# A shared PSUM bank in a seven-product down projection, and two transpose runs moved together in a stick-breaking head

## The chip, the cores and the metric

The kernel runs on one core of a Trainium2 chip. The metric is the device time of one execution, in microseconds (us). The core has TensorE (PE, matrix products and transposes, into the eight banks of PSUM), VectorE (DVE), ScalarE (ACT), GpSimd (POOL) and SyncE (SP, which issues the DMAs here). Each engine works through its own list of instructions in order and waits on semaphores for the others.

## The reference, cut to what matters

A decoder trunk of two layers, 512 tokens (T) of width 1024 (D), all in fp32. Each layer is FFN, mixer, FFN; the mixer of the first layer is a gated linear attention (GLA), that of the second a stick-breaking attention (SB).

```python
def swiglu(h, w_gate, w_up, w_down):
    return (silu(h @ w_gate) * (h @ w_up)) @ w_down      # 1024 -> 2816 -> 1024

def sb_mixer(h, w_in, w_out):            # 16 heads of 64
    q, k, v = split(h @ w_in, 3)
    # per head and block of 128 queries; mask is strictly causal
    z = (q_blk @ k.T) * scale
    sp = where(mask, softplus(z), 0)
    rem = reverse_cumsum(sp) - sp
    weights = where(mask, exp(log_sigmoid(z) - rem), 0)
    o = weights @ v
    return o @ w_out

for i in range(2):
    x = x + 0.5 * swiglu(rmsnorm(x), ...)
    x = x + mixer[i](rmsnorm(x))
    x = x + 0.5 * swiglu(rmsnorm(x), ...)
return rmsnorm(x)
```

## The kernel before, in words

**Number format.** A product in fp32 is made of three products of a shorter format. Each operand is split into a high half (a cast on ACT, `wh`, L129) and a low half (the rest, a subtraction on DVE, `wl`, L130); PE adds high by high, low by high and high by low into the same PSUM bank. Activations are split in the same way (`hh` and `hl`, L790 and L791; `xh` and `xl`).

**Layout.** x lies with features on the partitions, as eight tiles of 128 by 512. All eight PSUM banks are in one pool, under four tags with 2, 3, 2 and 1 banks (`a`, `z`, `t`, `o`). `psum(name)` without a tag (L46) goes round these eight in a fixed order, one turn for each call; `psum(name, tag)` takes the next bank of that tag. A bank that is taken again has to wait until its last reader is done.

**The order of the work.** The phases are FFN, GLA, FFN, FFN, SB, FFN. Weight products are entries of one queue, `feed`; an entry's body is a generator that yields at points where other work may be placed, and `feed.step(n)` goes on by n such points. Starting an entry also splits the weights of up to two further entries and asks for loads up to five ahead (`raw` and `rawd` are the tiles that a DMA from DRAM fills, two buffers each). On top of the order in the program text, a list scheduler places each engine's instructions; so an edit can move instructions that it doesn't name.

**FFN.** A part of the gate and up projections uses seven products of half size in place of eight (`seven`, product at L693). Its results pass through DVE: among others, the gate is multiplied in from PSUM (L706, `o <- ps_w, o`), then the result is split (L790, L791). A copy of a partial sum (`u`, L736) is made on ACT.

**Down by seven.** Two of the groups of 512 hidden features in each FFN (`DOWN_SEVEN = (1, 3)`) use seven products for the down projection too, in `seven_down` (L332 to 429). Each call makes a part (256 columns at two places) of the output; there are two parts in each group, so 16 calls in the four FFNs. Every product goes by `prod` (matmul at L372): two blocks of 128 by three, six matmuls with 256 columns, for each of two values of m. `add` (L376 to 378) adds the half of a finished sum into x, on DVE, straight from PSUM. `body_1` makes in this order: the products `b11` into two banks `ps_w`, and copies of them into two banks `ps_z` (ACT, L390); then `t1` into two banks `ps_q` (L391 to 394), with an `add` after each; then `t2`, `b21`. `body_2` adds `t3` to `ps_w`, `b22` to `ps_q` with an `add` after each, and `t4` to `ps_w`.

**SB.** `run` (L1394 to 1432) goes through 17 steps s, of which each does three things for heads, with steps of `feed` between them, an entry's step being for example twelve products of 512 columns (`ps_f`).

- `weights_log` for head s: in three blocks, the scores into `ps_z` (L1319, tag `z`), then on ACT Abs (L1338), Exp and Ln (`act`, L586) and Relu (L1341), on DVE a reverse scan (L1344) and a subtraction from `ps_z` (`r`, L1352). One `feed` step stands after the second block.
- `weights` for head s - 1 (L1355 to 1372): ten transposes of 128 by 128 (L1366) in three runs of 4, 4 and 2, each into a bank `ps_T` (tag `t`, two banks), each followed by an Exp on ACT that makes `wt` (L586). I call these exponentials exp a, b and c, and the runs T4, T4 and T2. A `feed` step stands after the first run and after the second, as long as the step has any left.
- `values` (L1374 to 1392), at every second step, for the pair of heads: 16 products into `ps_oT` (L1381) from the `wt` of both heads, a cast `oh` (L1390) and a subtraction `ol`.

ACT also splits the queries and keys of the next pair of heads (`mq`, L1292, and `kh`, L1303, from `n`).

Of the kernel before, what the change touches and what calls it, by code (L numbers as in the profile page):

```python
# [32 lines left out]
def decoder(ctx: ExitStack, tc: tile.TileContext, a: dict, out: bass.AP):  # L33
# [13 lines left out]
    def psum(name, tag=None):  # L47
        if tag is None:
            tag = order[turn_[0] % 8]
            turn_[0] += 1  # L50
        return pp.tile([P, T], F32, tag=tag, bufs=banks[tag], name=name)
# [284 lines left out]
    def seven_down(pool, w, r0, hs, part):  # L336

        H = T // 2  # L340
        lower, upper = (
            Chunk(w[r0 : r0 + 4 * P, c : c + 256].rearrange("(f p) c -> p f c", p=P), 4, 256)
            for c in (part * 256, 512 + part * 256)
        )
        lower.few = upper.few = True
        v = {}

        def halves():

            lo, up = (c.load().rearrange("p (c two) d -> p two c d", two=2) for c in (lower, upper))  # L350
            return lo[:, 0], lo[:, 1], up[:, 0], up[:, 1]

        def sums_12(_):
            a11, _, a21, a22 = halves()
            s = v["s12"] = pool().tile([P, 4, 256], F32, tag="s", bufs=4, name="s12")
            nc.vector.tensor_tensor(out=s[:, 0:2], in0=a21, in1=a22, op=ALU.add)
            nc.vector.tensor_tensor(out=s[:, 2:4], in0=s[:, 0:2], in1=a11, op=ALU.subtract)
            return s

        def sums_34(_):  # L360
            a11, a12, a21, _ = halves()
            s = pool().tile([P, 4, 256], F32, tag="s", bufs=4, name="s34")
            nc.vector.tensor_tensor(out=s[:, 0:2], in0=a11, in1=a21, op=ALU.subtract)
            nc.vector.tensor_tensor(out=s[:, 2:4], in0=a12, in1=v["s12"][:, 2:4], op=ALU.subtract)
            return s

        def prod(ps, w, k0, m, b, first):
            for c in range(2):
                bh, bl = hs[c][b]
                wh, wl = (t[:, k0 + c, m * P : (m + 1) * P] for t in w)  # L370
                for n, (l_, r_) in enumerate(((wh, bh), (wl, bh), (wh, bl))):
                    st["pe"] = nc.tensor.matmul(  # L372
                        ps, l_, r_, start=first and c + n == 0, stop=c == 1 and n == 2, skip_group_check=True
                    ).ins

        def add(m, up, col, ps):  # L376
            x = xs[part * 2 + m + 4 * up][:, col * H : col * H + H]
            nc.vector.scalar_tensor_tensor(out=x, in0=ps, scalar=0.5, in1=x, op0=ALU.mult, op1=ALU.add)

        def body_1(W):  # L380
            a11, s, v["a2"] = W
            ws, zs, qs = [], [], []
            for m in range(2):
                ws.append(psum("ps_w")[:, 0:H])
                prod(ws[m], a11, 0, m, "b11", True)
            for m in range(2):


                zs.append(psum("ps_z")[:, 0:H])
                nc.scalar.copy(zs[m], ws[m])  # L390
            yield  # L391
            for m in range(2):
                qs.append(psum("ps_q")[:, 0:H])
                prod(qs[m], s, 0, m, "t1", True)
                add(m, 1, 1, qs[m])
            yield
            for m in range(2):
                prod(ws[m], s, 2, m, "t2", False)
                add(m, 0, 1, ws[m])
            yield  # L400
            for m in range(2):
                prod(zs[m], v["a2"], 0, m, "b21", False)
                add(m, 0, 0, zs[m])
            v["w"], v["q"] = ws, qs
            yield

        def body_2(W):
            (s,) = W
            ws, qs = v["w"], v["q"]

            u3 = pool().tile([P, 2, H], F32, tag="c", bufs=1, name="u3")
            for m in range(2):
                prod(ws[m], s, 0, m, "t3", False)
                nc.scalar.copy(u3[:, m], ws[m])
                add(m, 1, 1, u3[:, m])
            yield
            for m in range(2):
                prod(qs[m], s, 2, m, "b22", False)
                add(m, 0, 1, qs[m])
            yield  # L420
            for m in range(2):
                prod(ws[m], v["a2"], 2, m, "t4", False)
                add(m, 1, 0, ws[m])
            yield

        units = [(lower, lambda t: halves()[0], 2, 256), (lower, sums_12, 4, 256), (lower, lambda t: halves()[1::2], 4, 256)]
        feed.q.append(Entry(units, body_1, NEAR, feed.q[-1].place != NEAR))
        assert not feed.q[-1].lead
        feed.q.append(Entry([(lower, sums_34, 4, 256)], body_2, NEAR))
# [55 lines left out]
    def stats_a(tag=None):  # L485

        if st["ss"] is None:
            sums = st["sums"]
        else:
            ps = psum("ps_st", tag)  # L490
            for i in range(NT):
                mm(ps[:, i : i + 1], st["ss"][:, i * P : (i + 1) * P], ones[:, 0:1], True, True)
            sums = ps[:, 0:NT]
        st["r4"] = rstd(sums, NT)
# [27 lines left out]
    def stats_b(tag=None):  # L522

        ps = psum("ps_R", tag)
        dgs = sp.tile([P, T], F32, tag="ss", name="dg")
        for i in range(NT):
            dg = dgs[:, i * P : (i + 1) * P]
            nc.vector.tensor_scalar(
                out=dg, in0=ident, scalar1=st["r4"][:, i : i + 1], scalar2=None, op0=ALU.mult
            )  # L530

            nc.tensor.matmul(
                ps[:, i * P : (i + 1) * P], ones, dg, start=i == 0, stop=i == NT - 1, skip_group_check=True
            )
        st["R"] = sp.tile([P, T], F32, tag="sq", name="R")
        nc.vector.tensor_copy(st["R"], ps)
# [24 lines left out]
    def two_halves(between=None):  # L561

        feed.finish()
        g = [feed.start(), feed.start()]
        for i in range(3):
            for x in g:
                next(x, None)
            if i == 0 and between is not None:
                between()

    def new_norm():
        st["h"], st["l"] = st["nh"], st["nl"]
# [684 lines left out]
    class SB:  # L1257
# [136 lines left out]
        def run(self):  # L1394
            with ExitStack() as es:
                vp = es.enter_context(tc.tile_pool(name="vp2", bufs=1, reuse_waits="tile"))
                self.op = es.enter_context(tc.tile_pool(name="op", bufs=8, reuse_waits="tile"))
                self.qp = es.enter_context(tc.tile_pool(name="qp2", bufs=4, reuse_waits="tile"))
                self.hp = es.enter_context(tc.tile_pool(name="hp3", bufs=2, reuse_waits="tile"))
                self.v = [vp.tile([P, D], F32, name=f"w{i}") for i in range(NT)]  # L1400
                self.ys, self.wt = {}, {}
                self.idb = vp.tile([P, P], BF16, name="idb")
                self.negm = vp.tile([P, P], BF16, name="negm")
                nc.vector.tensor_copy(self.idb, ident)
                nc.gpsimd.dma_start(self.negm, a["c_neg"])
                new_norm()
                two_halves()
                stats_a("t")
                feed.step(2)
                stats_b("t")  # L1410
                exp_ln_tables(st["sqrt"])
                flush(self.defer)
                feed.step(4)
                steps = [3] * 12 + [2, 1, 1, 2, 2]
                for s in range(17):
                    p, e = divmod(s, 2)
                    q, f = divmod(s - 1, 2)
                    n = steps[s]
                    if s < 16:
                        for i, _ in enumerate(self.weights_log(p, e)):  # L1420
                            if i == 1:
                                feed.step(1)
                                n -= 1
                    if s > 0:
                        for i, _ in enumerate(self.weights(q, f)):
                            if i < 2 and n > 0:
                                feed.step(1)
                                n -= 1
                        feed.step(n)
                        if f == 1:  # L1430
                            self.values(q)
                    else:
                        feed.step(n)
                feed.entries(self.end + 2 - feed.pos)
# [321 lines left out]
```

## Time and profile before

| | |
|---|---|
| median of 3 runs | 1836.07 us |
| lowest, highest | 1833.63, 1838.1 us |
| the profiled execution, its own time | 1833.41 us |
| its span in the trace | 1831.5 us |
| granted TensorE clock, mean | 0.999 |
| busy DVE, ACT | 84%, 58% |
| DMA, mean over the span | 98 GB/s |

The profile is of one execution. Each engine's busy time is a sum over its instructions. A matmul's length is modelled and contains the time until its result is there, while the next matmul may start long before that; so the distance from one start to the next tells what a product costs, and a pause on PE that is shorter than the rest of such a length is not in the list of waits. A row of the timeline has the start, the length, the engine, the line, the instruction, what it writes and reads, the shapes, and how many like it stand in a row; in brackets stands an idle time of the engine ahead of it, and what ended that.

### The profile page before, as it was taken

The numbers are of one execution on the slowest core, as the hardware profiler recorded it, in microseconds if no ns is written. First come the engines' busy times: TensorE is split into PE (matmuls) and PEld (weight loads), VectorE is DVE, ScalarE is ACT, GpSimd is POOL, SyncE is SP. The second block draws the span as 40 slices with busy tenths as digits, with TensorE's granted clock in tenths as the row PEclk, the third lists the DMA queues.
The fourth block names the chain that finished last, engine by engine and source line by source line (L and its number), as shares of the span: only waits on it lengthen the run. The fifth ranks groups of instructions, "written<-read, shape, count | busy, mean of one in ns | idle before, by whom it ended". The sixth has DMA issues, their size and how long they took to land.

```text
span 1831.5 us, 30847 instructions
## 1 busy us (share of the span) xinstructions
PE 1820.1 (99%) x12496; PEld 1657.0 (90%) x12496; DVE 1544.3 (84%) x2529; ACT 1058.7 (58%) x1856; POOL 8.8 (0%) x20
## 2 busy tenths in 40 slices
PE   9999999999999999999999999999999999999998
PEld 7999999889888899999889999998888788999997
DVE  8999798676787989889798988976878779898886
ACT  6556555544555556555555555555878755565554
POOL 0000000000000000000000000000000000000000
PEclk9999999999999999999999999999999999999999
DMA  5433333221123333333333333322222133233331
GB/s 163 137 115 106 104 116 117 79 70 55 62 69 115 93 115 100 120 104 104 99 98 115 93 115 116 104 82 81 70 70 64 64 92 115 93 116 104 104 121 53
DMA packets 177794, 179.22 MB, mean 98 GB/s; under 512 B 4146, under 2 KB 168292, under 8 KB 177652
## 3 DMA queue, kind: packets, MB, share of 16 engines
q1 hardware_dynamic: 176800, 175.91, 30.8%
q8 instruction: 98, 1.61, 0.4%
q0 software_dynamic: 608, 1.05, 0.2%
q14 instruction: 44, 0.36, 0.1%
q10 hardware_dynamic: 244, 0.29, 0.0%
HBM read 175.17 MB, written 2.10 MB: 97 GB/s over the span
## 4 chain that ended last, share of the span: by engine, by line
PE 94%; DVE 4%; ACT 1%; DMA 1%; issue 0%; SPq 0%; DVEq 0%; ACTq 0%
PE ps_w L693 21%; PE ps_f L66 18%; PE ps_d L66 16%; PE ps_q L693 10%; PE ps_z L693 5%; PE ps_t L66 5%; PE ps_w L372 4%; PE ps_b L66 4%; PE ps_q L372 2%; PE ps_S L66 1%; PE ps_z L1319 1%; PE ps_z L372 1%; PE ps_oT L1381 1%; DVE wl L130 1%; PE ps_bt L66 1%; PE ps_T L1366 1%
## 5 line engine op out<-in xcount | busy, mean ns | idle before, releaser
L130 DVE TENSOR_TENSOR wl<-raw,wh 128x512 fp32r<-128x512 f32 (+1 forms) x242 | 256.7, 1061 | 66.8 <-ACT wh L129 47.7
L129 ACT CAST wh<-raw 128x512 fp32r<-128x512 f32 (+1 forms) x242 | 223.5, 925 | 97.7 <-PE ps_f L66 32.8
L130 DVE TENSOR_TENSOR wl<-s,wh 128x1024 fp32r<-128x1024 f32 x176 | 214.6, 1220 | 46.9 <-PE ps_z L693 29.1
L129 ACT CAST wh<-s 128x1024 fp32r<-128x1024 f32 x176 | 184.2, 1047 | 109.5 <-DVE s L683 25.1
L693 PE MATMUL ps_w<-th,wh 128*128 128x256 f32 x864 | 239.5, 277 | 1.0 <-ACT u L736 0.9
L693 PE MATMUL ps_w<-tl,wh 128*128 128x256 f32 x864 | 238.7, 276 | 0.0
L693 PE MATMUL ps_w<-th,wl 128*128 128x256 f32 x864 | 238.7, 276 | 0.0
L66 PE MATMUL ps_f<-xh,wh 128*128 128x512 f32 x432 | 172.4, 399 | 0.0
L66 PE MATMUL ps_f<-xl,wh 128*128 128x512 f32 x432 | 169.3, 392 | 0.0
L66 PE MATMUL ps_f<-xh,wl 128*128 128x512 f32 x432 | 168.9, 391 | 0.0
L693 PEld LDWEIGHTS ps_w<-th,wh 128*128 128x128 f32 x864 | 162.4, 188 | 1.8 <-ACT u L736 1.3
L66 PE MATMUL ps_d<-hh,wl 128*128 128x512 f32 x416 | 162.2, 390 | 0.0
L66 PE MATMUL ps_d<-hh,wh 128*128 128x512 f32 x416 | 162.2, 390 | 0.0
L693 PEld LDWEIGHTS ps_w<-th,wl 128*128 128x128 f32 x864 | 162.2, 188 | 0.0
L693 PEld LDWEIGHTS ps_w<-tl,wh 128*128 128x128 f32 x864 | 162.2, 188 | 0.0
L66 PE MATMUL ps_d<-hl,wh 128*128 128x512 f32 x416 | 161.8, 389 | 0.0
L129 ACT CAST wh<-rawd 128x1024 fp32r<-128x1024 f32 (+1 forms) x100 | 82.9, 846 | 71.8 <-issue 31.8
L130 DVE TENSOR_TENSOR wl<-rawd,wh 128x1024 fp32r<-128x1024 f32 (+1 forms) x100 | 96.0, 963 | 16.4 <-PE ps_z L693 8.6
L327 DVE SCALAR_TENSOR_TENSOR x<-ps_d,x 128x512 f32<-128x512 f32 x120 | 81.2, 686 | 22.9 <-PE ps_d L66 22.5
L66 PEld LDWEIGHTS ps_f<-xl,wh 128*128 128x128 f32 x432 | 81.1, 188 | 17.3
L66 PEld LDWEIGHTS ps_f<-xh,wl 128*128 128x128 f32 x432 | 81.3, 188 | 15.7
L66 PEld LDWEIGHTS ps_f<-xh,wh 128*128 128x128 f32 x432 | 81.2, 188 | 15.3
(353 smaller groups left out, 5286.1 us busy)
## 6 DMA issues: line engine op xcount, KB each, us to landing
raw<-in_ffn_w_gate_dram SPq DMA_DIRECT2D x43, 1024.0 KB, 5.4
raw<-in_ffn_w_up_dram SPq DMA_DIRECT2D x43, 1024.0 KB, 5.4
rawd<-in_ffn_w_down_dram SPq DMA_DIRECT2D x84, 512.0 KB, 3.6
raw<-in_gla_w_in_dram SPq DMA_DIRECT2D x12, 1024.0 KB, 5.3
raw<-in_sb_w_in_dram SPq DMA_DIRECT2D x16, 512.0 KB, 3.8
raw<-in_gla_w_out_dram SPq DMA_DIRECT2D x4, 1024.0 KB, 4.9
raw<-in_sb_w_in_dram SPq DMA_DIRECT2D x4, 1024.0 KB, 5.2
raw<-in_sb_w_out_dram SPq DMA_DIRECT2D x4, 1024.0 KB, 5.0
```

Source lines behind the costliest of these rows:

```text
L66: st["pe"] = nc.tensor.matmul(ps, l, r, start=first, stop=last).ins
L129: st["cut"] = nc.scalar.copy(h[:, k], part).ins
L130: nc.vector.tensor_tensor(out=l[:, k], in0=part, in1=h[:, k].bitcast(F32), op=ALU.subtract)
L327: nc.vector.scalar_tensor_tensor(out=xs[k], in0=ps, scalar=0.5, in1=xs[k], op0=ALU.mult, op1=ALU.add)
L372: st["pe"] = nc.tensor.matmul(ps, l_, r_, start=first and c + n == 0, stop=c == 1 and n == 2, skip_group_check=True).ins
L693: st["pe"] = nc.tensor.matmul(o, l_, r_, start=first and j + n == 0, stop=j == 3 and n == 2, skip_group_check=True).ins
L1319: nc.tensor.matmul(o_, l_, r_, start=first, stop=last, skip_group_check=True)
L1366: nc.tensor.transpose(ps[:, c0 : c0 + P], ys[yb][:, yc + j * P : yc + (j + 1) * P], ident)
L1381: nc.tensor.matmul(po[e * 64 : e * 64 + 64, j * P : T], self.v[j][:, c : c + 64], self.wt[p, e][bk][:, c0 : c0 + n], start=j == 0, stop=j ...
```

## The change

In `seven_down`, the two `t1` products go into the two halves of one bank, which takes one turn of `psum` where there were two. The start flag is set for the first product alone. The two additions stand after both products and no longer one after each. In `body_2` the additions of `b22` are moved behind both products likewise.

In SB's `run`, the `feed` step after the first run of transposes is taken out, so that the first two runs, T4 and T4, follow each other. The step after the second run stays. The step that was taken out is made after the third run instead, since what is left of the steps is made there (`feed.step(n)`), ahead of `values`.

```diff
             yield
+
+            ps = psum("ps_q")
             for m in range(2):
-                qs.append(psum("ps_q")[:, 0:H])
-                prod(qs[m], s, 0, m, "t1", True)
+                qs.append(ps[:, m * H : (m + 1) * H])
+                prod(qs[m], s, 0, m, "t1", m == 0)
+            for m in range(2):
                 add(m, 1, 1, qs[m])
             yield
...
             for m in range(2):
                 prod(qs[m], s, 2, m, "b22", False)
+            for m in range(2):
                 add(m, 0, 1, qs[m])
             yield
...
                         for i, _ in enumerate(self.weights(q, f)):
-                            if i < 2 and n > 0:
+                            if i == 1 and n > 0:
                                 feed.step(1)
                                 n -= 1
                         feed.step(n)
```

Lines of the changed kernel stand 3 further down between the two edits of `seven_down` and 4 further behind them: L1366 is L1370 there, L586 is L590.

## The prediction

> **What bounds the kernel now.** I read the page first, for the bound; then TensorE's waits, for what stops it; then the timeline at the two places that the change touches.
>
> ```profile
> span 1831.5 us, 30847 instructions
> ...
> PE 1820.1 (99%) x12496; PEld 1657.0 (90%) x12496; DVE 1544.3 (84%) x2529; ACT 1058.7 (58%) x1856; POOL 8.8 (0%) x20
> ...
> PE 94%; DVE 4%; ACT 1%; DMA 1%; issue 0%; SPq 0%; DVEq 0%; ACTq 0%
> ```
>
> TensorE (PE) is busy for 99% of the span and carries 94% of the chain that ended last. An edit therefore counts only by what it does to the time between two starts on PE; time on DVE or ACT counts where PE waits for it. The busy figure hides small stalls, because a product's length is a modelled latency and the next one starts before it ends. The list of waits shows only what is left beyond that modelled end:
>
> ```profile
> PE ps_q L372 <- DVE o L706: 1.1, 4, 0.3
> ...
> PE ps_w L693 <- ACT u L736: 0.9, 2, 0.7
> ...
> PE ps_oT L1381 <- ACT wt L586: 0.2, 1, 0.2
> ```
>
> The largest entry is the wait that the first part of the change is about, the third one belongs to the second part. Both are small, and both are larger from start to start.
>
> **Part 1, one bank for the two ps_q products of down by seven.** Before, the second product (L393, matmul L372) takes a bank of its own, whose last reader was the gate multiplication on DVE (L706) of the seven-product projection ahead of it. First and last of the four large losses, and one of the two small ones:
>
> ```profile
> 254.20 0.28 PE L372 MATMUL ps_q<-hh,wl 128*128 128x256 f32 x1
> 254.31 0.28 PE L372 MATMUL ps_q<-hl,wh 128*128 128x256 f32 x1
> 254.88 0.38 PE L372 MATMUL ps_q<-hh,wh 128*128 128x256 f32 x1 [0.29 <-DVE o L706]
> 255.10 0.29 PE L372 MATMUL ps_q<-hh,wl 128*128 128x256 f32 x1
> ```
> ```profile
> 1615.56 0.28 PE L372 MATMUL ps_q<-hl,wh 128*128 128x256 f32 x1
> ...
> 1616.35 0.28 PE L372 MATMUL ps_q<-hh,wl 128*128 128x256 f32 x1
> ```
> ```profile
> 851.58 0.28 PE L372 MATMUL ps_q<-hl,wh 128*128 128x256 f32 x1
> ...
> 852.02 0.28 PE L372 MATMUL ps_q<-hh,wl 128*128 128x256 f32 x1
> ```
>
> The pitch of undisturbed products is 0.11 us (254.20 to 254.31). Two pitches, 0.23, should lie between the last product of the first half and the second of the next; there are 0.79 (254.31 to 255.10; the same at 1615.56), which loses 0.56, and 0.44 at 851.58, which loses 0.21. Sixteen calls of down by seven run; four lose 0.56 and two 0.21: **2.66 us**. In the changed kernel the second product needs no bank, so this wait goes. Every later bank comes round one turn later or at the same turn, never earlier: what is late next can be at most the same DVE work, at a bank taken later.
>
> What is added: both additions (L378) now follow both products, because bank and reader are one. DVE's row for them:
>
> ```profile
> 256.61 0.75 DVE L378 SCALAR_TENSOR_TENSOR x<-ps_q,x 128x256 f32<-128x256 f32 x2
> ```
>
> Where DVE is late, as here, nothing changes: the pair starts at 256.61, after both products had ended anyway. Where it is on time, the first addition loses its place beside the second product and the pair ends one addition (0.75 / 2 = 0.37 us) later. Behind it on DVE are the subtractions that make the weights' low halves (L130), which are made an entry ahead, so I put this at nothing; if that cover failed in the ten calls in which DVE is on time, it would be 3.7 us. Below nothing it can't be: no work is taken off DVE. Value taken: **-2.7**, ends -2.7 and +1.0 (3.7 - 2.7).
>
> [...]
>
> **Part 2, the transposes of a stick-breaking head.** Before, each head goes four transposes (T4), twelve products, T4, twelve products, T2, and then, for every second head, the sixteen products of `values` (ps_oT). After: T8, twelve, T2, twelve, `values`. Number of instructions and their forms are unchanged on every engine; only order moves, and no DMA is issued earlier or later by the edit itself.
>
> Does adjacency pay by itself? Rows of head 4 and of the one place where six transposes already stand together:
>
> ```profile
> 1322.07 0.61 PE L1366 MATMUL ps_T<-ident,r 128*128 128x128 f32 x4
> 1322.44 0.47 PE L66 MATMUL ps_f<-xh,wh 128*128 128x512 f32 x1
> ...
> 1325.29 0.60 PE L1366 MATMUL ps_T<-ident,r 128*128 128x128 f32 x4
> ```
> ```profile
> 1424.31 0.81 PE L1366 MATMUL ps_T<-ident,r 128*128 128x128 f32 x6
> 1425.05 1.72 PE L1381 MATMUL ps_oT<-wt,w 128*64 128x512 f32 x6
> ```
>
> Four take 0.37 until the next start, six take 0.74. So a run costs about 0.11 each, and the break between runs costs about nothing. Adjacency as such: 0.
>
> What pays is what now stands elsewhere. (a) T2 was directly ahead of `values`; now products are. (b) On ACT, the exponentials of the second and third run move ahead of casts, as the order of the two built kernels shows, and `values` waited for them:
>
> ```profile
> 1304.33 2.38 PE L1381 MATMUL ps_oT<-wt,w 128*64 128x512 f32 x16
> 1306.64 0.44 PE L1319 MATMUL ps_z<-kh,mq 128*128 128x384 f32 x1
> ```
> ```profile
> 1328.50 0.38 PE L1366 MATMUL ps_T<-ident,r 128*128 128x128 f32 x2
> 1328.81 2.94 PE L1381 MATMUL ps_oT<-wt,w 128*64 128x512 f32 x16
> 1331.68 0.44 PE L1319 MATMUL ps_z<-kh,mq 128*128 128x384 f32 x1
> ```
> ```profile
> 1378.30 2.97 PE L1381 MATMUL ps_oT<-wt,w 128*64 128x512 f32 x16
> 1381.20 0.44 PE L1319 MATMUL ps_z<-kh,mq 128*128 128x384 f32 x1
> ...
> 1381.91 0.28 PE L1319 MATMUL ps_z<-kl,mq 128*128 128x256 f32 x1
> ```
> ```profile
> 1429.33 0.39 PE L1319 MATMUL ps_z<-kh,mq 128*128 128x256 f32 x1
> ```
>
> (a) Two transposes take 0.31 until `values` (1328.50 to 1328.81) where two runs' pitches are 0.22: 0.09 in each of eight heads, -0.7. (b) The sixteen products take 2.31 undisturbed (1304.33 to 1306.64), 2.87 at 1328.81 and 2.90 at 1378.30: -0.56 and -0.59. At 1425.05 they are broken in two with five ps_z products between, and the next starts at 1429.33: 4.28, less 2.31, less about 0.83 for the five (1381.20 to 1381.91 and one pitch): -1.14. Together **-3.0**.
>
> What it costs: ps_T has two banks, so each run takes the bank of the run two before it, and T2 that of its own head's first run: it waits until ACT has read that (exp a, L586). Before, 24 products lay between the two; now twelve do. Behind T2 on PE wait twelve products that need nothing from it, and behind those the next head's ps_z. The list of waits of before has no such wait, so its price comes from where exp a ends:
>
> ```profile
> 1286.65 0.61 PE L1366 MATMUL ps_T<-ident,r 128*128 128x128 f32 x4
> ...
> 1297.64 0.61 PE L1366 MATMUL ps_T<-ident,r 128*128 128x128 f32 x4
> ...
> 1385.67 0.61 PE L1366 MATMUL ps_T<-ident,r 128*128 128x128 f32 x4
> ```
> ```profile
> 1292.37 1.07 ACT L586 ACTIVATE wt<-ps_T 128x512 f32<-128x512 f32 x2
> ```
> ```profile
> 1302.58 0.61 ACT L586 ACTIVATE wt<-ps_T 128x512 f32<-128x512 f32 x1
> ```
> ```profile
> 1319.06 1.05 ACT L129 CAST wh<-raw 128x1024 fp32r<-128x1024 f32 x1 [2.80 <-DMA raw<-in_sb_w_in_dram]
> ...
> 1321.30 0.38 ACT L586 ACTIVATE wt<-ps_T 128x256 f32<-128x256 f32 x1
> ...
> 1326.36 0.61 ACT L586 ACTIVATE wt<-ps_T 128x512 f32<-128x512 f32 x1
> ```
> ```profile
> 1389.36 0.58 ACT L586 ACTIVATE wt<-ps_T 128x512 f32<-128x512 f32 x1
> ```
>
> T2 is wanted 3.22 (T4 and twelve, 1322.07 to 1325.29) and 0.44 (four more) = 3.66 us after the first transpose; in head 1, where fifteen products lie between, 0.70 later. Head 1: wanted 1291.01, exp a ends at 1292.96 (half of the pair): 1.95. Head 4: wanted 1325.73, exp a ends 1326.97, less 0.28 because the third exponential (1321.30) no longer stands ahead of it: 0.96. Head 9: wanted 1389.33, ends 1389.94: 0.61. Heads 5 and 8 repeat 9 and 4, since the work on ACT repeats (the DMA wait of 2.8 too). Head 2 ends at 1303.19 - 0.28, wanted 1301.30: 1.6, but PE comes 1.95 later than before by then while ACT there is still working off its queue, so nothing. In the other heads exp a ends ahead of T2. Sum 1.95 + 2 x 0.96 + 2 x 0.61 = **+5.1**. Ends: 0, if ACT comes earlier, and 7.6 (rival 1).
>
> **Sum.** -2.7 - 3.0 + 5.1 = -0.6 us on 1833.41 us, the profiled execution's own time (its span of 1831.5 and 1.9 around it). That execution lies 2.66 below the median of the runs, 1836.07; on the median it gives **1835.5 us**. The rest of the order moves little; the wait for u (0.9 us in the list above) can go either way by that much.
>
> **The rivals**, on the median. About 0.2%, 3.7 us, is what a measurement can tell from no change.
>
> 1. *T2's bank wait takes more than is saved* (slower). If ACT falls back with PE, because what feeds exp a are PE's own ps_z products, nothing is absorbed in head 2 and nothing gained by the earlier third exponential: 1.95 + 1.88 + 2 x 1.24 + 2 x 0.61 = 7.6, and the exponentials stay behind, so (b) isn't had: 7.6 - 0.7 - 2.7 = +4.2, **1840.3**. It decides from exp a ending more than 3.66 us after the head's first transpose. For it: ACT's wait for a DMA just ahead of heads 4 and 8. Against: ACT is busy only 58%.
> 2. *T2 finds its bank free* (faster). After head 1 PE is 1.95 us late, and if DMA and ACT are not, every later exp a has that margin, more than the 0.96 wanted: +0 to 1.95 - 2.7 - 3.0 = -5.7 to -3.7, middle **1831.4**. For it: the cast at 1319.06 waits for a DMA and not for PE. Against: the DMA's buffer is freed by work that follows PE.
> [...]
> 4. *Part 1 doesn't do what it says*: the wait for L706 only moves to the next bank. The sum without its 2.7 is +2.1, **1838.2**.
>
> **How the numbers follow.** Forecast 0.40, rival 1 0.32, rival 2 0.22, rivals 3 and 4 0.03 each. Rival 1 is the one slower, rival 2 the one faster, the rest lie within 0.2%: 0.22, 0.46, 0.32. The forecast's own range is 1833 to 1838. The range reaches to both big rivals: down to 1830 (lower end of rival 2, 1830.4) and up to 1842 (1840.3, and about 1.9 for the ends of part 1's unknown and u).
>
> **What would show it.** Right, part 1: no wait of ps_q for L706, starts in both halves 0.11 apart, L378 in pairs. Right, part 2: `values` at 2.3 us in all heads, and T2 waiting for wt (L586) in heads 1, 4, 5, 8, 9 with about 2.0, 1.0, 0.6, 1.0, 0.6. [...] A time off by more than this with the same waits would mean that the new order moved something far from both edits.

## The result, and the profile after

The change makes the kernel slower by a little.

| | before | after |
|---|---|---|
| median of 22 runs each | 1836.63 us | 1839.88 us |
| lowest to highest | 1833.63 to 1841.2 us | 1836.04 to 1843.8 us |
| ratio to before, 95% interval | | 1.0016 [1.0009, 1.0023] |
| the profiled execution, its span | 1833.41, 1831.5 us | 1840.37, 1838.6 us |

+3.25 us by the medians, 0.16% by the ratio. The two profiled executions lie 7.1 us apart in their spans, more than twice that; more on this below.

The page of the changed kernel, its first lines and the chain that ended last:

```profile
span 1838.6 us, 30829 instructions
...
PE 1823.1 (99%) x12496; PEld 1660.7 (90%) x12496; DVE 1544.0 (84%) x2529; ACT 1058.9 (58%) x1856; POOL 8.8 (0%) x20
...
PE 91%; ACT 3%; DVE 3%; DMA 1%; SPq 0%; issue 0%; DVEq 0%; ACTq 0%
```

Every engine has as many instructions as before; ACT has 3% of the chain where it had 1%. The first two entries of the list of PE's waits:

```profile
PE ps_T L1370 <- ACT wt L590: 4.7, 5, 1.9
PE ps_z L1323 <- DVE r L1356: 1.6, 1, 1.6
```

The ps_q entry is gone, and so is that for u. In their place stand five waits of the transposes for an exponential, which the prediction had named, and one of ps_z for r, which it had not. The first and the last of the five in the timeline of PE:

```profile
1292.00 0.39 PE L66 MATMUL ps_f<-xl,wh 128*128 128x512 f32 x1
1294.27 0.44 PE L1370 MATMUL ps_T<-ident,r 128*128 128x128 f32 x2 [1.88 <-ACT wt L590]
```
```profile
1394.26 0.39 PE L66 MATMUL ps_f<-xl,wh 128*128 128x512 f32 x1
1395.16 0.44 PE L1370 MATMUL ps_T<-ident,r 128*128 128x128 f32 x2 [0.52 <-ACT wt L590]
```

A product of 512 columns is followed after 0.23 us; here it takes 2.27 and 0.90, so 2.04 and 0.67 are lost, and with the three between 5.5 us.

And the two ps_q products of down by seven that lost 0.56 us at 254.31:

```profile
256.24 0.28 PE L372 MATMUL ps_q<-hl,wh 128*128 128x256 f32 x1
256.36 0.28 PE L372 MATMUL ps_q<-hh,wh 128*128 128x256 f32 x1
256.47 0.28 PE L372 MATMUL ps_q<-hh,wl 128*128 128x256 f32 x1
```
```profile
258.53 0.75 DVE L378 SCALAR_TENSOR_TENSOR x<-ps_q,x 128x256 f32<-128x256 f32 x2
```

They run through at 0.11 us from start to start. The additions are a pair as before, 0.75 us.

**Two paces of PE.** Of the 7.1 us between the spans, 4.8 stand in streams of products with 256 columns, which ran at two paces in these profiles. The same 9 us of work in the first FFN, in the view of stretches (from and to, length in us, then busy time and instructions of PE, PEld, DVE, ACT, POOL, then the granted clock, the DMA's share and GB/s), after and before:

```profile
148.40:157.40 9.00, 9.00 (x82) 9.00 (x81) 8.48 (x14) 5.17 (x10) 0.00 (x0) 1.00 0.30 96
158.40:167.40 9.00, 9.00 (x78) 9.00 (x78) 8.71 (x15) 5.19 (x9) 0.00 (x0) 1.00 0.36 116
```
```profile
158.40:167.40 9.00, 9.00 (x82) 9.00 (x82) 8.90 (x15) 6.05 (x10) 0.00 (x0) 1.00 0.37 117
```

There are 82 products in 9 us in before and, ten us earlier, in after, and 78 from 158.4 on in after, at a granted clock of 1.00 in all three, and with no pause in between. From start to start it is 113.4 ns or 117.8 ns, 3.9% more. I call a run of the latter a slow stretch. There are three in before's profile (445 to 458, 1155 to 1191, 1557 to 1572), nine in after's, 13 to 26 us long. A stretch costs its length times 4.4/117.8, the 4.4 ns being the difference of the two paces: 2.4 us in all in before, 7.2 in after. Without them the two executions lie 2.3 us apart, split at the first ps_z and the last ps_oT product of the stick-breaking stage (below: the stage): -1.5 ahead of the stage, +5.4 in it (188.9 to 194.2 us), -1.6 behind it.

### The profile page after: what moved, and what is told of

It reads as the page before. It is cut to its first block, busy times and chain, and to the rows that moved or that the text cites. A ratio compares the mean times of both kernels' runs of the same rounds, so it can differ in the third digit from the quotient of the medians.

```text
span 1838.6 us, 30829 instructions
## 1 busy us (share of the span) xinstructions
PE 1823.1 (99%) x12496; PEld 1660.7 (90%) x12496; DVE 1544.0 (84%) x2529; ACT 1058.9 (58%) x1856; POOL 8.8 (0%) x20
## 3 DMA queue, kind: packets, MB, share of 16 engines
q8 instruction: 98, 1.61, 0.4%
q0 software_dynamic: 608, 1.05, 0.2%
## 4 chain that ended last, share of the span: by engine, by line
PE 91%; ACT 3%; DVE 3%; DMA 1%; SPq 0%; issue 0%; DVEq 0%; ACTq 0%
PE ps_w L697 22%; PE ps_d L66 16%; PE ps_f L66 14%; PE ps_q L697 11%; PE ps_z L697 5%; PE ps_w L372 5%; PE ps_b L66 4%; PE ps_t L66 4%; PE ps_q L372 2%; PE ps_S L66 1%; PE ps_z L372 1%; PE ps_oT L1385 1%; PE ps_bt L66 1%; ACT l L590 1%; DVE l L1348 1%; PE ps_o L66 1%
```

## The experiments

The question was which part costs what, whether the wait of T2 is the price of part 2, where the 3.0 us went that part 2 was to bring, and what the slow stretches are. Each ratio is to the kernel before, run on the same chip at the same time; the runs are of three chips, so times are compared by these ratios and differences. "Slow" is the sum over the slow stretches of that profile.

| run | ratio, 95% interval | stage, us | slow, us |
|---|---|---|---|
| part 1 alone | 0.9990 [0.9982, 0.9999] | 188.7 | 5.4 |
| part 2 alone | 1.0025 [1.0015, 1.0035] | 196.0 | 2.2 |
| both, T2 in another bank | 0.9990 [0.9981, 0.9999] | 188.2 | 8.1 |
| before again | 1.0001 [0.9992, 1.0010] | 188.8 | 3.5 |
| additions moved, two banks | 0.9998 [0.9989, 1.0007] | 188.8 | 1.5 |
| part 1 and an extra product | 1.0148 [1.0130, 1.0167] | 188.8 | 17.0 |
| T2 in another bank, old order in the tail | 0.9981 [0.9972, 0.9990] | 188.8 | 2.1 |
| part 1, bank turn kept | 0.9985 [0.9976, 0.9994] | 188.9 | 3.0 |
| after again | 1.0023 [1.0013, 1.0032] | 195.9 | 2.7 |
| part 2 alone again | 1.0030 [1.0019, 1.0041] | 195.8 | 1.5 |

**Part 1 alone.** After, with the step between the transposes put back:

```diff
-                            if i == 1 and n > 0:
+                            if i < 2 and n > 0:
```

> Part 1 of the change alone (one bank for both ps_q products, additions behind both); the transposes as before. By the traces of before and after, with the time of PE split at the first ps_z product of the stick-breaking stage and at its last ps_oT, and with the stretches taken off in which products of 256 columns start 117.8 ns apart in place of 113.4 (2.4 us in before, 7.2 in after), part 1 is worth 1.5 us ahead of that stage and 1.6 behind it. Theory: no wait of ps_q for L706, stage as before (188.9 us), 3 us faster than before, ratio 0.998 to 0.999. Rival: DVE's work is what really limits there, PE waits for it a little later (ps_w L693, 0.11 us a time) and falls into the slow pitch more often; then not faster at all, 0 to +2 us, with five or more slow stretches.

1833.28 against 1835.62 us, -2.3. No wait of ps_q, the stage as before. Without its slow stretches the profile is 4 to 5 us shorter than before's two profiles without theirs; the time shows half of that. Part 1 pays; the rival falls, though its slow stretches were there (six, 5.4 us).

**Part 2 alone.** Before, with only the line in `run`:

```diff
-                            if i < 2 and n > 0:
+                            if i == 1 and n > 0:
```

> Part 2 alone (T4 and T4 adjacent); down by seven as before. Theory: the stick-breaking stage takes 194.2 us as in after (188.9 before), T2 waits for wt in heads 1, 4, 5, 8 and 9 with 1.9, 1.1, 0.7, 1.0 and 0.7 us, the six ps_q waits are there (2.7 us); 5.4 us slower than before, ratio 1.003. Rival: the stage's loss comes in part from the bank rotation that part 1 shifts by a turn for each call; then the stage takes less than 193.

1839.99 us, +4.4 where 5.4 was expected. The ps_q waits are there (2.6 us), T2's five too. The stage takes 196.0, longer than in the changed kernel, not shorter, so the rotation of banks was not what cost there. Of the extra 1.8 us, 1.6 stand right behind the wait of head 1, where the granted clock is lower. The same place in part 2 alone and in after, by stretches:

```profile
1291.00:1293.20 2.20, 0.33 (x3) 0.06 (x2) 2.14 (x4) 2.15 (x5) 0.00 (x0) 1.00 0.00 0
1293.20:1296.70 3.50, 3.50 (x10) 2.82 (x11) 2.41 (x3) 0.76 (x2) 0.00 (x0) 0.53 0.51 150
1296.70:1300.00 3.30, 3.30 (x27) 2.97 (x27) 2.65 (x4) 2.68 (x5) 0.00 (x0) 0.99 0.00 0
```
```profile
1294.30:1298.00 3.70, 3.70 (x22) 3.12 (x23) 3.52 (x6) 1.97 (x4) 0.00 (x0) 1.00 0.50 142
```

Behind a wait of 1.87 us in part 2 alone the granted clock was 0.53 for 3.5 us, behind one of 1.88 us in after 1.00. Products of 512 columns started 0.43 us apart in the former, in place of 0.23.

**Both parts, T2 in another bank.** After, the third run in the one bank of tag o:

```diff
-                ps = psum("ps_T", "t")
+                ps = psum("ps_T", "o" if bk == 2 else "t")
```

> After, with the third run of transposes (T2) put into the one bank of tag o in place of the tag t, so that it doesn't have to wait for exp a of its own head; values of the pair takes that bank next, after exp c has read it, twelve products later. Theory, bank wait is the price: no wait of T2 for wt, and the stage falls by about 5.4 us, to 189 (if the gains of order foreseen for values are not there) or to 186 (if they are and the waits hid them); with part 1 3 to 6 us faster than before. Rival, ACT's lateness is the price: the wait moves to values (ps_oT for wt) or to the next ps_z, and the stage stays over 192.

1833.50 us, -2.1, less than the 3 to 6 expected: from 1.0016 to 0.9990 by the choice of a bank. The head of its list of waits of PE:

```profile
PE ps_z L1323 <- DVE r L1356: 1.4, 1, 1.4
PE ps_f L1627 <- DVE gT L58: 0.9, 1, 0.9
PE ps_oT L1385 <- ACT wt L590: 0.7, 2, 0.5
```

No ps_T for wt, and the stage is 6.0 us shorter than in after. So the wait for the bank was the price, and the rival falls: most of PE's wait doesn't come back elsewhere. But a part does: `values` now waits for wt. The wait of ps_z for r was there in after too (1.6 us), so it doesn't come from T2's bank. The stage is 188.2, near the expectation without gains of order, and not 186.

**Before again**, and **after again**, **part 2 alone again**, all unchanged:

> The kernel before once more, unchanged, for a second profile of it. Theory, falling into the slow pitch is chance: stretches at 117.8 ns at other places than in the first profile (445, 1154 and 1557 us), their sum other than 2.4 us by 1 or more, and the span other by as much, the q waits and the stage (188.9) within 0.3 of the first. Rival, the program fixes them: the same three places, 2.4 us.

> The changed kernel once more, unchanged. Theory: T2's five waits as in its first profile (together 5.4 to 5.6 us), the stage 194.2 us, or 195.8 if the granted clock falls to about half for 3.5 us behind the wait of head 1, as it did in part 2 alone (0.53 there, 1.00 in the first profile of this kernel); the slow pitch at places and with a sum that differ from the first profile (7.2 us) by 1 or more. Rival: the same stretches and the same sum, so that the slow pitch belongs to part 1.

> Part 2 alone once more, unchanged. Theory, the half clock behind the wait of head 1 is chance, set by when the wait falls: the stage 194.3 us without it, 196.0 with it; T2's waits the same. Rival: it belongs to this kernel (the wait stands 1.1 us earlier there than in the changed kernel), again 0.53 and 196.0.

Before: 1.0001, stage and ps_q waits (2.5 us) as at first, five slow stretches, none of them over one of the first profile's three but for a microsecond at 1557, 3.5 us in all in place of 2.4, and a span 2.1 us longer. After: T2's waits the same, two slow stretches in place of nine, 2.7 us in place of 7.2, and the granted clock fell behind head 1's wait (stage 195.9, as expected for that case). Part 2 alone: it fell again (stage 195.8). So both the slow stretches and the clock behind that wait differ between executions of the same program. The places of the stretches aren't free either: of the eleven profiles without the extra product below, ten have one that begins some 85 to 96 us behind the stage. The clock fell in three of four profiles with that wait, in the changed kernel too, so my rival for part 2 alone falls.

What the expectation called chance goes along with where the wait falls, in these four profiles. In the three, the clock falls at 1291.39 (after again), 1293.38 and 1293.65 us (part 2 alone, twice), is back 3.41 us later, and falls again 542.7 us behind the first fall, when PE has ended its work; 542.7 is 159 times 3.413. From these times alone it is my estimate that the clock was set anew in steps of 3.413 us. In after's first profile it falls only at the end, at 1835.36; 159 such steps ahead of that is 1292.64, in the middle of head 1's wait (1292.39 to 1294.27). The steps around that wait, two of after's first profile, then the one ahead of the fall in part 2 alone:

```profile
1289.23:1292.64 3.41, 3.16 (x14) 2.25 (x12) 3.35 (x8) 1.71 (x4) 0.00 (x0) 1.00 0.00 0
1292.64:1296.06 3.42, 1.79 (x9) 1.53 (x10) 3.33 (x4) 2.42 (x5) 0.00 (x0) 1.00 0.43 120
```
```profile
1289.97:1293.38 3.41, 1.54 (x9) 0.99 (x7) 3.35 (x6) 2.64 (x5) 0.00 (x0) 1.00 0.01 2
```

The wait is the same 1.9 us in all four. In the three that fell, 1.86 or 1.87 us of it lie in one step; in the fourth it was cut into 0.25 and 1.62. Part 2 alone again also has 1.61 us idle in one step, at ps_z, and the clock didn't fall there; nor did it behind the last product of the run with the old order in the tail (below), with 1.86 us in one step. So about 1.86 us idle in one step went with a fall in three profiles and without one in that run; what decides isn't shown.

**The additions moved, two banks.** Before, with the additions behind both products only:

```diff
                 prod(qs[m], s, 0, m, "t1", True)
+            for m in range(2):
                 add(m, 1, 1, qs[m])
...
                 prod(qs[m], s, 2, m, "b22", False)
+            for m in range(2):
                 add(m, 0, 1, qs[m])
```

> Before, with the additions of t1 and b22 behind both products (as in the change), but with two ps_q banks as before; transposes as before. Theory, the shared bank is what pays in part 1: the six waits of ps_q for L706 stay (2.5 to 2.7 us), same time as before, ratio 0.999 to 1.001. Rival, the new place of the additions on DVE pays: ps_q waits fall below 1 us and the time falls by 2 us. The two waits of ps_w for u (L736, 0.93 us each from start to start), which went in part 1 alone too, tell whether they go by this or by the bank's turn.

0.9998. Both waits are as before:

```profile
PE ps_q L372 <- DVE o L708: 1.1, 4, 0.3
...
PE ps_w L695 <- ACT u L738: 0.9, 2, 0.7
```

The new place of the additions neither costs nor pays; the shared bank does.

**Part 1, bank turn kept.**

```diff
             ps = psum("ps_q")
+            turn_[0] += 1
```

> Part 1 alone, with one turn of the bank rotation left out after the shared bank, so that every later bank is the same as before. Theory, the ps_q waits go because no bank is taken for the second product: none of them here either; the two waits for u (0.93 each) go or stay with the order that the scheduler makes, and with them 1.8 us. Ratio to before 0.998 to 0.9995. Rival, the rotation itself pays: ps_q waits or others of 0.5 us and more for L706 come back at another bank, and the time is that of before.

1832.54 us, 0.9985. No ps_q waits, but the two for u are back:

```profile
PE ps_w L698 <- ACT u L741: 1.3, 2, 0.7
```

So the shared bank pays without the shift of the rotation. The two u waits, up to 0.93 us each from start to start, follow the rotation: with it shifted, the scheduler puts the copy u ahead of a cast of weights that waits for DVE, as the rows of ACT show in before and in part 1 alone:

```profile
660.92 1.05 ACT L129 CAST wh<-s 128x1024 fp32r<-128x1024 f32 x1 [1.59 <-DVE s L677]
661.88 0.36 ACT L736 COPY u<-ps_w 128x256 f32<-128x256 f32 x1
```
```profile
660.68 0.37 ACT L740 COPY u<-ps_w 128x256 f32<-128x256 f32 x1 [1.03 <-PE ps_w L697]
661.23 1.05 ACT L129 CAST wh<-s 128x1024 fp32r<-128x1024 f32 x1 [0.18 <-DVE s L681]
```

In time the two kernels can't be told apart (0.9990 and 0.9985).

**Part 1 and an extra product.** In each `seven`, ahead of the second product:

```diff
+                nc.tensor.matmul(v["q"], s[0][:, 0, 0:P], st["h"][0], start=True, stop=True, skip_group_check=True)
                 prod(q, s, 0, lambda j: self.t_half(0, j))
```

> Part 1 alone, with one extra product of 512 columns in each seven-product projection, ahead of its second product (its result is overwritten, the output is the same). 72 times 0.23 us, so about 16 us longer. Theory, the slow pitch (117.8 ns) begins at a short wait inside a stream of products of 256 columns and lasts until products of 512 columns come: then no slow stretch goes on past the next extra product, they are 4 us long or less inside the projections, where part 1 alone had 16 to 33 us. Rival, the slow pitch is a state of the clock with a length of its own: stretches of 16 us and more as before.

1862.92 us, by two runs: 27.9 above before and some 30 above part 1 alone, where 16 was expected. The extra products take their 16.4 us (72 times 0.227), and the slow stretches take 17.0 where part 1 alone had 5.4. Two stretches of it, each between one extra product and the next:

```profile
69.30:78.70 9.40, 9.40 (x82) 9.40 (x81) 9.40 (x15) 6.25 (x13) 0.00 (x0) 1.00 0.49 164
79.30:88.70 9.40, 9.40 (x85) 9.40 (x84) 6.69 (x11) 5.29 (x9) 0.00 (x0) 1.00 0.31 98
```

In this run the extra product didn't end the slow pace, it switched it: of 72, all 48 that came at 113.4 ns were followed by 117.8, and all 24 that came at 117.8 by 113.4. My theory is right that slow stretches ended at such a product, and wrong that it only ends them; a projection is also 9 us long and not 4, so the stretches are. The rival, a state of the clock with a length of its own, falls: the pace changed at every one of the 72, at a granted clock of 1.00.

**T2 in another bank, and the old order in the tail.**

```diff
-                            if i == 1 and n > 0:
+                            if (i == 1 if s < 12 else i < 2) and n > 0:
...
-                ps = psum("ps_T", "t")
+                ps = psum("ps_T", "o" if bk == 2 and p < 6 and (p, e) != (5, 1) else "t")
```

> Part 1, and for the steps up to 11 part 2 with the third run of transposes in the bank of tag o; from step 12 on, where few products are left, the order of the transposes of before. Theory, the foreseen gains at values (0.57 and 0.59 us) are real and what took them back is the tail (a wait of ps_z for r of 1.4 us) and two waits of values for wt (0.6 and 0.2): the stage takes about 188.0 us or a little less, against 188.2 with part 2's order to the end and 188.9 before; the time 2 to 4 us below before. Rival, the tail's wait doesn't come from the order but from work pushed back: stage 189 or more.

1832.17 us, 0.9981, the lowest ratio of all. The wait of ps_z for r is back at before's 0.4, but the stage is 188.8, so between my two cases. One block of `values` is late here that was not late in before, that of head 2:

```profile
1303.03 0.28 PE L66 MATMUL ps_t<-wh,xl 128*128 128x256 f32 x1
1303.86 0.65 PE L1385 MATMUL ps_oT<-wt,w 128*64 128x512 f32 x2 [0.56 <-ACT wt L590]
```

Start to start 0.83 where after has 0.21, so 0.62 is lost. The blocks of heads 4 and 8, which took 2.87 and 2.90 us in before, run 2.30 us long here and start 0.10 late each. So up to head 11 the new order without T2's wait gains less than 0.1 us in all: 1.0 in heads 4 and 8, against 0.7 lost in head 2 and 0.16 each in heads 6 and 10. With the tail's order of before, its 1.14 isn't gained. That it beats part 1 alone isn't shown: the intervals overlap, the stage is equal, and its profile has 3.3 us less in slow stretches.

## Why the prediction was right or wrong, point by point

The forecast was 1835.5 us, 0.6 below before; it came out 3.25 above. The measured 1839.88 us lies within the wide range of 1830 to 1842, which reached to both big rivals, but outside the forecast's own 1833 to 1838, and the sign of the likeliest sum was wrong.

- **Part 1, -2.7: right in mechanism.** All six waits went, no later bank took them (rival 4 out), and the additions cost nothing (0.9998 in the run with only the additions moved, so rival 3, that they reach PE, is out). In time part 1 alone was -2.3 and, with the turn kept, -2.5. That two u waits went as well, I hadn't seen: I had left u open either way.
- **Adjacency at 0: right.** A run of eight takes 0.80 us until the next start in after, two of four took 0.36 and 0.35. Behind each run the first product takes 0.31 us until the next start in place of 0.23, about 0.08 more, and there is one such run less, which makes up for the 0.09.
- **T2's bank wait, +5.1: right.** Heads 1, 4, 5, 8 and 9 waited, no other up to head 12, with 2.0, 1.1, 0.7, 1.0 and 0.7 us, 5.5 in all. Head 2 was absorbed as argued. With another bank the stage fell by 6.0. Rival 2 is out; so is rival 1 as it stood, with waits in head 2 and more at 4 and 8. That the time came near its 1840.3 is luck: its terms weren't met, and they add up to 7.5 and not to its 7.6.
- **What pays, -3.0: the step that failed.** It came to about nothing: the stage is 5.4 us longer, and T2's wait alone is 5.5. Of (a), -0.7, nothing was had. The 0.09 us don't belong to T2 but to the entry of `values`, with either kind of product ahead: in after it starts 0.32 us behind a product of 512 columns (1332.99 to 1333.31) in place of 0.23, and 0.21 behind one of 256 (1307.51 to 1307.72) in place of 0.11. In before, transposes stood ahead of `values` in every head, so its rows couldn't tell the two apart. With T2's wait and (b) taken off, heads 2, 4, 6, 8 and 10 came out 0.04 to 0.15 longer, not 0.09 shorter. Of (b), the blocks of `values` at heads 4 and 8 did get 0.57 and 0.60 shorter, and that at head 12 is whole. Six rows of after and the row of r, then the same place in before:

```profile
1332.99 0.39 PE L66 MATMUL ps_f<-xl,wh 128*128 128x512 f32 x1
1333.31 2.37 PE L1385 MATMUL ps_oT<-wt,w 128*64 128x512 f32 x16
1335.61 0.44 PE L1323 MATMUL ps_z<-kh,mq 128*128 128x384 f32 x1
...
1433.69 0.45 PE L1323 MATMUL ps_z<-kh,mq 128*128 128x384 f32 x1
...
1438.16 1.04 PE L1370 MATMUL ps_T<-ident,r 128*128 128x128 f32 x8
1440.81 0.41 PE L1323 MATMUL ps_z<-kh,mq 128*128 128x384 f32 x1 [1.60 <-DVE r L1356]
```
```profile
1440.13 0.53 DVE L1356 TENSOR_TENSOR r<-ps_z,l 128x384 f32<-128x384 f32 x1
```
```profile
1426.70 0.45 PE L1319 MATMUL ps_z<-kh,mq 128*128 128x384 f32 x1
...
1427.89 1.51 PE L1381 MATMUL ps_oT<-wt,w 128*64 128x384 f32 x10 [0.21 <-ACT wt L586]
...
1433.07 1.04 PE L1366 MATMUL ps_T<-ident,r 128*128 128x128 f32 x8
1434.27 0.41 PE L1319 MATMUL ps_z<-kh,mq 128*128 128x384 f32 x1 [0.17 <-DVE r L1352]
```
```profile
1433.59 0.53 DVE L1352 TENSOR_TENSOR r<-ps_z,l 128x384 f32<-128x384 f32 x1
```

  At head 12 the gain is 1.0 us, and one head later 1.45 come back (2.65 us from the transposes to ps_z in place of 1.20; 0.45 of it was lost a few products further on in before, so 1.0 in all). ps_z takes a bank that r has yet to read, and the chain from head 13's scores to the end of r runs on ACT and DVE. That chain is no longer than before: 7.0 us in after (1433.69 to 1440.66), 7.4 in before (1426.70 to 1434.12). But in before these scores stood ahead of the last ten products of `values`, and in after they stand behind all sixteen, so PE has that much less to do until it needs the bank. What I had counted as a stall at head 12 was time in which this chain ran. From step 12 on two steps of products a head or fewer are left to lie between. I counted the stall that went and didn't ask there what is late next. The stage comes to +5.4 without the clock's fall: 5.5 for T2, -1.2 at `values` of heads 4 and 8, -1.0 in head 12, +1.0 in head 13, +0.5 in small waits of the last transposes, and the rest (+0.6) in steps of 0.15 us or less over the other heads, most of it in those with `values`.
- **Not in the sum at all: the clock.** Behind the wait of head 1, 1.9 us long in all four profiles with it, the granted clock fell in three, to 0.53 over 3.5 us in part 2 alone, for 1.6 us more; in after's first it stayed at 1.00. That the place of the wait decided is my estimate from these four alone: 1.86 or 1.87 us of it in one step of 3.41 us in the three, 0.25 and 1.62 in two steps in the fourth.
- **The sum.** Part 2 alone was +4.4 and, again, +6.1 us by the medians, where I had +2.1; with part 1 at -2.3 that gives 2.1 and 3.8, where both parts together measured +3.25 and, again, +4.2. What stays open is how much of part 1's 4 to 5 us the slow stretches take back on average: with shifted rotation the profiles have 7.2, 2.7, 5.4, 8.1 and 2.1 us, without it 2.4, 3.5, 2.2, 1.5, 3.0 and 1.5. That looks like more, but the same kernel gave 7.2 and 2.7.

## What to carry to other kernels

A wait can be worth removing by sharing a bank, and another can be made by moving two users of a ring of two banks closer together: count how much work lies between the release and the reuse, before and after. A delay between two groups of rows may belong to the second of them and go along with it, so look for a place where something else stands ahead of that one. Where a stall on the bound engine goes, follow that engine to its next wait on the engines that were never late before; the gain is what is left there. Behind a new wait of 1.9 us the granted clock fell in three of four profiles here, for 1.6 us more, so add such a fall to the price of a like wait as a chance, and where kernels differ by some 2 us, take more than one profile of each before reading a span.

## What the runs showed of the hardware that I had not expected

PE's products of 256 columns ran at two paces in these profiles, 113.4 and 117.8 ns from start to start, at a granted clock of 1.00; a cast of 1024 columns on ACT took 1.04 to 1.05 us beside either. In the run with the extra products, each of these products of 512 columns switched between them, 72 times of 72. A short wait went with a switch too, at one place: behind a wait of 0.11 us the pace went to 117.8 in after, and in before such a wait at the same place left it at 113.4. After's rows at 158 us:

```profile
157.78 0.28 PE L697 MATMUL ps_q<-tl,wh 128*128 128x256 f32 x1
157.89 0.39 PE L697 MATMUL ps_w<-th,wh 128*128 128x256 f32 x1
158.11 0.28 PE L697 MATMUL ps_w<-th,wl 128*128 128x256 f32 x1
```

The wait costs 0.11 us (157.89 to 158.11 is 0.22, in place of 0.11), the 26 us behind it 0.98. What decides whether a wait switches the pace wasn't tried.
